# Two thirds of an attention's value projection moved ahead of its queries and keys, and made by a seven-product scheme

## The chip, the cores and the metric

The kernel runs on one core of a Trainium2 chip. The metric is device time in microseconds (us) of one execution. Engines in this text: PE (TensorE, matrix products), DVE (VectorE), ACT (ScalarE) and SP, whose queue issues the loads of weights. PE writes into PSUM, which has eight banks here (the tile `banks`, 128 x 8 x 512); DVE and ACT read results from there.

## The reference

A two-layer encoder on 256 tokens of width 2048, all in float32. Only the second layer's attention changes; in short:

```python
def dilated_attention(h, w_qkv, w_o):        # h: (1, 256, 2048)
    qkv = (h @ w_qkv).reshape(B, T, G, 3, DIL_HEADS, HEAD_DIM)   # G=3 groups, 8 heads of 128
    for g, (window, dil) in enumerate(((128, 1), (512, 4), (2048, 16))):
        q = apply_partial_rotary(qkv[:, :, g, 0], cos, sin) * (HEAD_DIM ** -0.5)
        k = apply_partial_rotary(qkv[:, :, g, 1], cos, sin)
        v = qkv[:, :, g, 2]
        o, lse = banded_attention(split(q), split(k), split(v), n_side)
        ...
    wts = softmax(stack(lses), axis=0)
    return (sum of wts * outs).reshape(B, T, 1024) @ w_o
```

`x = x + dilated_attention(rms_norm(x, g))` stands between two feed-forward blocks `x + relu(h @ w1)**2 @ w2` with 8192 hidden columns. The merge over groups equals one softmax over the 512 score columns of the three groups together, and the kernel does it so.

## The kernel before

**Float32 products from three.** Every float32 operand is split into a high part (rounded to the fp32r type) and a low part, the rest. `three` (lines 197 to 201) issues high*high, high*low, low*high. For weights the high part `wh` is a cast by ACT (L194) and the low part `wl` a subtraction by DVE (L195), each over half a step's weights, 128 x 1024.

**Steps.** The program is a list of steps; each takes one 128 x 2048 block of weights (1 MB, 512 rows by 512 columns, or 256 by 1024) and has four quarters of matmuls. The list is walked by hand in order, and every engine runs its instructions in that order. In step `i`, after each quarter `n`: the PE part of the tasks put at that quarter, the `after` list, then `prep(i + 2, n)` (which makes the parts of the weights of step `i + 2`), then the tasks' DVE and ACT work (`post`). At the end of a step come `evac`, `prep(i + 2, 3)`, `load(i + 5)` on SP and the step's `post`. `wh` and `wl` have four buffers each, so the half made in step `i` for step `i + 2` goes where a half of step `i` has just been read.

Three kinds of steps matter:

- Column form (`gemm_cols`, kind "a"): queries and keys, transposed. The weights are the stationary operand; a step issues 16 matmuls of 512 columns with `wh` (L229) and 16 of 256 with `wl` (L234). In the first step of a projection the `wl` products of quarters 2 and 3 each read both halves; in the middle ones quarter 2 reads the first half and quarter 3 the second.
- Row form (`gemm_rows`, kind "a"): values and the output projection, 24 matmuls of 512 columns.
- Pairs (`gemm_pair`): the feed-forward. A step takes 256 rows by 1024 columns. Kind "s" issues eight products by `three`, 24 matmuls. Kind "x" issues seven, by a scheme in Strassen's manner, 21 matmuls, from sums of weight blocks that DVE makes in `prep_x` (lines 166 to 188) and sums of activation blocks (`sums_and_parts`). Five banks more take part, and at the end of a call the sums are closed on DVE (`begin`, `last_sum`).

**The second attention.** After the first feed-forward, for each half `hh` of the eight heads: 24 column steps (queries and keys of the three groups, four steps each), then 12 row steps (values of the three groups). Then eight row steps of the output projection. `DilHeads` has the head tasks, for each of the four heads `h` of a half:

- `s1`: scores into a bank; its post adds the mask (L908) into `sc` and, for group 2, runs `softmax` (reduce L659, two exponentials on ACT L662, reciprocal L664, scaling L666).
- `s2`: eight transposes (L918, L920) into two banks; its post splits them on ACT and DVE (`dpT`, `dpTd`).
- `s3`: products with the values (L199 to L201 with `dpT`, then L940); its post writes `oT`, ACT L950 and then DVE L951.

In "a" steps a task's bank comes from `Banks.misc`, which hands out banks 6 and 7 in turn. With `i` the first step after the last key projection of a half, `s1` of group 2 stands at steps `i + 2` to `i + 5`, `s2` at `i + 7` to `i + 10`, `s3` at `i + 12` and `i + 13`. After each query or key projection come its turns (rotary, DVE L865 to L868): the first half at the end of the projection's last step, the second at quarter 1 of the next.

**The norm ahead of it.** `Norm` transposes chunks of `x` (L393) and scales them into `xT`; pairs 4 to 7 (chunks 2 and 3) come last, in the last step of the feed-forward and the first of the attention. With `perm` tokens are put in another order, and DVE makes the low part by `gx` (L421) and a subtraction (L423). `rows` and `rows_out` (L454), then `cols` and `cols_out`, one step apart, spread the reciprocal root; `cols` reads what `rows_out` wrote.

Of the kernel before, what the change touches and what calls it, by code (L numbers as in the profile page):

```python
# [14 lines left out]
P = 128  # L15
T = 256
# [32 lines left out]
def tile_encoder(ctx: ExitStack, tc: tile.TileContext, ins, out):  # L49
# [242 lines left out]

    def gemm_pair(w, cp, A, sums_of, order, finish, split_end=False, soon=False):
        made, q = [], {}
# [3 lines left out]
        def left(pair, which):  # L298

            t, u = A[pair // 2], 2 * (pair % 2)  # L300
            names = ("S3", "S2", "S4", "S1")[:sums_of[pair].shape[2]] if pair in sums_of else ()
            if which in names:
                c = sums_of[pair]
                return [c[:, h, names.index(which), :] for h in range(2)]
            a, ts_ = {"A11": (0, 0), "A12": (1, 0), "S1": (0, 1), "A21": (0, 1), "A22": (1, 1)}[which]
            return [t[:, u + a, h, ts_ * P:(ts_ + 1) * P] for h in range(2)]
# [67 lines left out]
    class Norm:  # L374
        def __init__(self, n, perm, pairs=(), kept=()):
            self.n, self.perm, self.kept = n, perm, kept
# [18 lines left out]
        def parts(self, c, half, halves=(0, 1)):  # L395
# [3 lines left out]
            if 2 * c + half in self.pairs:  # L399
                keep = int(2 * c + half in self.kept)  # L400
                raw = blocks()
                for a in range(2):
                    k = 4 * c + 2 * half + a
                    nc.scalar.activation(raw[:, 3 + 2 * a:5 + 2 * a, :].rearrange("p u t -> p (u t)"), self.tp[:, a, :], AF.Copy, scale=gT[:, self.n, k:k + 1])
                self.sums[2 * c + half] = part.pool.tile([P, 2, 3 + keep, P], F32R, name="xs", tag=("xs", "xk")[keep],
                                                              bufs=1 if keep else len(self.pairs) - len(self.kept))
                sums_and_parts(raw, xT, half, self.sums[2 * c + half])
                return
            for which, a in [(which, 2 * half + a) for which in ("hi", "lo") for a in halves]:
# [15 lines left out]
                else:  # L425
                    nc.vector.scalar_tensor_tensor(out=lo, in0=src, scalar=g, in1=hi.bitcast(F32),
                                                   op0=ALU.mult, op1=ALU.subtract)

        def root(self):
# [39 lines left out]

    def sums_and_parts(b, t, half, sums):  # L470

        hi, lo = (t[:, 2 * half:2 * half + 2, h, :].rearrange("p a (u t) -> p a u t", u=2) for h in range(2))
        whole = b[:, 3:7, :].rearrange("p (a u) t -> p a u t", u=2)
        keep = sums.shape[2] == 4

        def own():
            nc.scalar.copy(hi, whole)
            subtract(nc.vector, lo, whole, hi.bitcast(F32))

        if keep:  # L480
            own()
# [3 lines left out]
        if not keep:  # L485
            nc.scalar.copy(hi, whole)
        for n, src in ((slice(0, 3), b[:, 0:3, :]), (slice(3, 4), b[:, 4:5, :]))[:1 + keep]:
            nc.scalar.copy(sums[:, 0, n], src)
        if not keep:
            subtract(nc.vector, lo, whole, hi.bitcast(F32))  # L490
        for n, src in ((slice(0, 3), b[:, 0:3, :]), (slice(3, 4), b[:, 4:5, :]))[:1 + keep]:
            subtract(nc.vector, sums[:, 1, n], src, sums[:, 0, n].bitcast(F32))

# [43 lines left out]
    def at_after(i, n, f):  # L537
        later_after.append((i, n, f))
# [172 lines left out]
    def ffn(norm, w1, w2, next_norm, next_done):  # L711
        for g in range(4):
# [4 lines left out]
            def hidden(made, q, cp, hT=hT, sums=sums, pairs2=pairs2, last=last):  # L717
# [14 lines left out]
                for r in range(4):  # L732
# [10 lines left out]
                    def post(r=r, held=held):  # L743
# [3 lines left out]
                        if pair in pairs2:  # L747
# [3 lines left out]
                            def parts_of(c=c, half=half, raw=raw, pair=pair):  # L751
                                sums[pair] = part.pool.tile([P, 2, 3, P], F32R, name="hs", tag="hsum", bufs=3)
                                sums_and_parts(raw, hT[c], half, sums[pair])
                            steps[i + (3 if cp else 2 * r - 1)].after[1].append(parts_of)
# [6 lines left out]
            for cp in range(2):  # L761
                more = g and not cp
                order = ff_order(FF_PAIRS + FF_KEPT, (0, 1, 2, 5, 3, 4, 6, 7)) if more else ff_order(FF_PAIRS)
                gemm_pair(w1, 2 * g + cp, norm.xT, norm.sums, order, lambda made, q, cp=cp: hidden(made, q, cp))

# [49 lines left out]
            for cp in range(2):  # L815
                parted = last and cp == 1
                order = range(8) if last else (0, 1, 2, 4, 3, 6, 5, 7)
                if parted:
                    order = ((0, 1, 2, 4, 3, 5, 6, 7), (0, 1, 3, 2, 5, 4, 6, 7))[next_done is None]
                gemm_pair(w2g, cp, hT, sums, ff_order(pairs2, order), lambda made, q, cp=cp, parted=parted: residual(made, q, cp, parted),  # L820
                          parted, parted and next_done is not None)

    ffn(norms[1], ins["ffn0_w1"], ins["ffn0_w2"], lambda: norms[2], begin_norm(2, True))


    parts[len(steps)] = "attention"
    n2 = norms[2]
    dil_oT = [None] * 2
    rope = {}
# [20 lines left out]
    class DilHeads:  # L850
        def __init__(self, hh):
            self.hh = hh
            self.q, self.k, self.v, self.sc = {}, {}, {}, {}

# [25 lines left out]
        def v_out(self, g, acc):  # L880
            if g == 0:
                self.v[g] = split_v(acc, n2.r)
                return
            t = part.pool.tile([P, 2, 512], F32, name="v", tag="mid", bufs=9)
# [45 lines left out]
        def s3_pe(self, h):  # L930
# [4 lines left out]
            for kt in range(2):  # L935
                three(o[:, 0, :], [v[:, kt, hs] for v in self.v[0]], [hi[:, kt, :], lo[:, kt, :]], kt == 0, False)
            for g in (1, 2):
# [14 lines left out]

    wd = ins["dil_wqkv"]
    at(len(steps), None, load_rope)
    at(len(steps) + 2, None, make_rope)
    for hh in range(2):
# [3 lines left out]
        for g in range(3):  # L960
# [16 lines left out]

# [214 lines left out]
```

## Time and profile before

| | us |
|---|---|
| median of 3 runs | 2254.18 (2252.92 to 2256.74) |
| the profiled execution | 2253.24 |
| its span, first to last instruction | 2251.5 |

| stretch of the span (us) | what | PE busy | DVE busy | ACT busy |
|---|---|---|---|---|
| 640 to 1080 | first feed-forward, later part | 440.00 | 414.85 | 264.56 |
| 1080 to 1220 | queries and keys, half 0 | 140.00 | 106.53 | 61.79 |
| 1220 to 1290 | values, half 0 | 70.00 | 48.19 | 38.37 |
| 1290 to 1440 | queries and keys, half 1 | 150.00 | 101.06 | 62.86 |
| 1440 to 1510 | values, half 1 | 70.00 | 46.77 | 37.32 |

How to read it: busy time is the time in which an engine had at least one instruction in flight. Successive matmuls overlap, so a single one's duration (0.39 us for 512 columns) is longer than the distance from one to the next (0.23 us); the chain of work shows distances, the timeline durations. A timeline row has the start, the duration, engine and line, operation, what is written and read, and in brackets the idle time of the engine before it and what ended it. A row of windows has the stretch, its length, the busy time of PE, weight loads, DVE, ACT and POOL, the granted PE clock, DMA share and GB/s.

### The profile page before, as it was taken

To read this page: it belongs to the slowest core of one execution; us is meant where nothing else is said; L and a number is where in the kernel's file an instruction comes from. 1 tells how busy PE (TensorE), PEld (TensorE's weight loads), DVE (VectorE), ACT (ScalarE), POOL (GpSimd) and SP (SyncE) were. 2 spreads that over 40 slices of the span, in tenths; PEclk is the share of its full clock that TensorE was granted. 3 is DMA by queue.
4 is the path that set the end of the run, shared out by engine and by line. 5 is a ranking of instruction groups with operands and counts; after the bars stand their busy time and mean duration, and the time that the engine had idled before them with its cause. 6 is when DMAs were issued, how large, how long until landed. Compare 5 with 4: busy or idle time off the path is not lost.

```text
span 2251.5 us, 28385 instructions
## 1 busy us (share of the span) xinstructions
PE 2238.7 (99%) x10906; PEld 1883.4 (84%) x10906; DVE 1891.8 (84%) x2217; ACT 1269.2 (56%) x1582; POOL 0.7 (0%) x6
## 2 busy tenths in 40 slices
PE   9999999999999999999999999999999999999998
PEld 8888888888888888888888888888888888888886
DVE  6776666899999999989877667757999999999988
ACT  6555455665665565565444544456665665665664
POOL 0000000000000000000000000000000000000000
PEclk9999999999999999999999999999999999999999
DMA  7556554656656666665555445444666666666664
GB/s 256 177 186 192 177 180 165 203 187 209 202 188 207 200 192 206 196 190 190 209 180 186 170 169 183 172 169 151 208 201 197 199 205 192 200 204 192 204 218 136
DMA packets 110728, 430.33 MB, mean 191 GB/s; under 512 B 23872, under 2 KB 24448, under 8 KB 92160
## 3 DMA queue, kind: packets, MB, share of 16 engines
q1 hardware_dynamic: 109920, 426.82, 58.1%
q8 instruction: 85, 1.39, 0.2%
q10 hardware_dynamic: 672, 1.70, 0.2%
q14 instruction: 51, 0.42, 0.1%
HBM read 426.38 MB, written 2.10 MB: 190 GB/s over the span
## 4 chain that ended last, share of the span: by engine, by line
PE 98%; DVE 1%; ACT 1%; issue 0%; ACTq 0%; POOLq 0%; POOL 0%; DVEq 0%
PE banks L199 25%; PE banks L201 25%; PE banks L200 25%; PE banks L229 13%; PE banks L234 7%; PE banks L740 1%; PE banks L393 1%; PE banks L940 0%; PE banks L900 0%; PE banks L635 0%; PE banks L1072 0%; PE banks L918 0%; PE banks L920 0%; ACT wh L194 0%; DVE wl L195 0%
## 5 line engine op out<-in xcount | busy, mean ns | idle before, releaser
L195 DVE TENSOR_TENSOR wl<-w,wh 128x1024 fp32r<-128x1024 f32 (+1 forms) x802 | 963.1, 1217 | 235.0 <-ACT wh L194 148.3
L194 ACT CAST wh<-w 128x1024 fp32r<-128x1024 f32 (+1 forms) x802 | 824.6, 1048 | 457.0 <-PE banks L201 306.3
L199 PE MATMUL banks<-wh,xT 128*128 128x512 f32 x1074 | 423.3, 394 | 0.0
L200 PE MATMUL banks<-wl,xT 128*128 128x512 f32 x1074 | 418.7, 390 | 0.0
L201 PE MATMUL banks<-wh,xT 128*128 128x512 f32 x1074 | 418.5, 390 | 0.0
L199 PE MATMUL banks<-wh,hT 128*128 128x512 f32 x804 | 316.2, 393 | 0.0
L201 PE MATMUL banks<-wh,hT 128*128 128x512 f32 x804 | 313.2, 390 | 0.0
L200 PE MATMUL banks<-wl,hT 128*128 128x512 f32 x804 | 312.9, 389 | 0.0
L229 PE MATMUL banks<-xT,wh 128*128 128x512 f32 x1280 | 312.5, 392 | 0.0
L229 PEld LDWEIGHTS banks<-xT,wh 128*128 128x128 f32 x1280 | 233.4, 188 | 44.2 <-ACT wh L194 0.2
L180 ACT CAST hs<-sums 128x1536 fp32r<-128x1536 f32 x98 | 145.3, 1482 | 186.5 <-DVE sums L138 186.5
L201 PEld LDWEIGHTS banks<-wh,xT 128*128 128x128 f32 x1074 | 201.6, 188 | 42.2
L200 PEld LDWEIGHTS banks<-wl,xT 128*128 128x128 f32 x1074 | 201.9, 188 | 40.6 <-DVE wl L195 1.2
L199 PEld LDWEIGHTS banks<-wh,xT 128*128 128x128 f32 x1074 | 201.9, 188 | 39.7
L201 PEld LDWEIGHTS banks<-wh,hT 128*128 128x128 f32 x804 | 150.9, 188 | 31.6
L200 PEld LDWEIGHTS banks<-wl,hT 128*128 128x128 f32 x804 | 151.1, 188 | 30.3
L135 DVE TENSOR_TENSOR ls<-sums,hs 128x1536 fp32r<-128x1536 f32 x98 | 171.6, 1751 | 5.6 <-ACT hs L180 5.6
L199 PEld LDWEIGHTS banks<-wh,hT 128*128 128x128 f32 x804 | 151.0, 188 | 30.0
L234 PE MATMUL banks<-xT,wl 128*128 128x256 f32 x1280 | 172.7, 284 | 0.1
L234 PEld LDWEIGHTS banks<-xT,wl 128*128 128x128 f32 x1280 | 165.8, 191 | 6.6 <-DVE wl L195 0.6
L138 DVE TENSOR_TENSOR sums<-w 128x1024 f32<-128x1024 f32 x98 | 119.4, 1218 | 0.0
L199 PE MATMUL banks<-wh,oT 128*128 128x512 f32 x192 | 76.6, 399 | 0.0
(186 smaller groups left out, 2348.7 us busy)
## 6 DMA issues: line engine op xcount, KB each, us to landing
w<-in_ffn_w_dram SPq DMA_DIRECT2D x512, 512.0 KB, 4.7
w<-in_dil_wqkv_dram SPq DMA_DIRECT2D x72, 1024.0 KB, 4.8
w<-in_na_wqkv_dram SPq DMA_DIRECT2D x47, 1024.0 KB, 5.2
w<-in_na_wo_dram SPq DMA_DIRECT2D x16, 1024.0 KB, 4.8
w<-in_dil_wo_dram SPq DMA_DIRECT2D x8, 1024.0 KB, 4.7
bias<-in_rpb_dram SPq DMA_DIRECT2D x32, 96.0 KB, 10.0
out_dram<-x SPq DMA_DIRECT2D x8, 256.0 KB, 2.6
x<-in_x_dram SPq DMA_DIRECT2D x3, 512.0 KB, 9.0
```

The source lines that it names most:

```text
L135: engine.tensor_tensor(out=out, in0=a, in1=b, op=ALU.subtract)
L138: engine.tensor_tensor(out=out, in0=a, in1=b, op=ALU.add)
L180: nc.scalar.copy(s.hs, s.sums)
L194: nc.scalar.copy(dst_hi, src)
L195: nc.vector.tensor_tensor(out=dst_lo, in0=src, in1=dst_hi.bitcast(F32), op=ALU.subtract)
L199: nc.tensor.matmul(o, left[0], right[0], start=start, stop=False)
L200: nc.tensor.matmul(o, left[0], right[1], start=False, stop=False)
L201: nc.tensor.matmul(o, left[1], right[0], start=False, stop=stop)
L229: nc.tensor.matmul(acc[j // 2][:, j % 2, :], s.hi[a][:, j * P:(j + 1) * P], xT[k][:, a].rearrange("p h t -> p (h t)"), start=k == 0 and a ...
L234: nc.tensor.matmul(acc[j // 2][:, j % 2, :T], s.lo[a][:, j * P:(j + 1) * P], xT[k][:, a, 0, :], start=False, stop=k == nk - 1 and a == 3)
L393: nc.tensor.transpose(self.tp[:, a, tb * P:(tb + 1) * P], x[:, tb, kt * P:(kt + 1) * P], ident)
L740: nc.tensor.transpose(t[:, a, tb * P:(tb + 1) * P], q["C"][:, 2 * tb + f // 4, f % 4 * P:(f % 4 + 1) * P], ident)
```

## The change

The values of 16 of the 24 value steps move to the front of the second attention, as two calls of `gemm_pair` of eight steps each: the group 0 values of both halves (weight blocks 4 and 5), then the values of half 0 for groups 1 and 2 (blocks 10 and 16). In the first call pairs 5 and 6 are "x" steps, in the second 5, 6 and 7: five in all. The eight steps left are the row-form values of half 1 for groups 1 and 2. `gemm_pair` takes the list of its two column blocks.

```diff
+    gemm_pair(wd, (4, 5), n2.xT, n2.sums, ff_order((5, 6), (0, 1, 2, 3, 5, 4, 6, 7)), two_groups)
+    gemm_pair(wd, (10, 16), n2.xT, n2.sums, ff_order((5, 6, 7), (0, 1, 2, 5, 3, 6, 7, 4)), one_half)
+
+    s0 = len(steps)
+    parts[s0 + 1] = "attention"
+    at(s0 + 1, None, load_rope)
+    at(s0 + 2, None, make_rope)
...
-        for g in range(3):
-            acc = {}
-            made = gemm_rows(wd, g * 3072 + 2048 + hh * 512, n2.xT, range(4), acc, 0, 3)
-            made[-1].evac.append(lambda H=H, g=g, acc=acc: H.v_out(g, acc))
+        if hh:
+            for g in (1, 2):
+                acc = {}
+                made = gemm_rows(wd, g * 3072 + 2048 + hh * 512, n2.xT, range(4), acc, 0, 3)
+                made[-1].evac.append(lambda H=H, g=g, acc=acc: H.v_out(g, acc))
```

The values are written by `two_groups` (`high` on ACT, `low` on DVE, within the next call's first steps) and `one_half` (ACT):

```diff
+        for m, (tb, hh) in enumerate(QUARTERS):
+            made[-1].after[m].append(lambda tb=tb, hh=hh: last_sum(q, tb, hh, q["C"][:, 2 * tb + hh, :]))
+            at_after(i, m, lambda tb=tb, hh=hh: high(tb, hh))
+            at_after(i + (m + 1) // 4, (m + 1) % 4, lambda tb=tb, hh=hh: low(tb, hh))
```

The head tasks get steps and quarters of their own, counted from `i = begins[2]`, the first step after the half's last key projection. For half 0 these steps are now the column steps of half 1, for half 1 its eight row steps and the output projection:

```diff
+        i = begins[2]
+        S1, S2, S3 = ((((1, 1), (2, 1), (5, 1), (6, 1)), ((4, 1), (6, 3), (8, 1), (9, 1)), ((6, 1), (8, 3), (10, 1), (11, 1))),
+                      (((1, 1), (2, 1), (3, 1), (4, 1)), ((4, 3), (5, 1), (6, 1), (7, 1)), ((8, 1), (8, 3), (9, 1), (9, 3))))[hh]
...
-                at(begins[g] + 2 + h, lambda H=H, h=h, g=g: H.s1_pe(h, g), lambda H=H, h=h, g=g: H.s1_post(h, g))
+                when, n = S1[h] if g == 2 else (2 + h, 1)
+                at(begins[g] + when, lambda H=H, h=h, g=g: H.s1_pe(h, g), lambda H=H, h=h, g=g: H.s1_post(h, g), quarter=n)
...
-            at(begins[2] + 7 + h, lambda H=H, h=h: H.s2_pe(h), lambda H=H, h=h: H.s2_post(h))
-            at(begins[2] + 12 + h // 2, lambda H=H, h=h: H.s3_pe(h), lambda H=H, h=h: H.s3_post(h),
-               quarter=(1, 3)[h % 2])
+            at(i + S2[h][0], lambda H=H, h=h: H.s2_pe(h), lambda H=H, h=h: H.s2_post(h), quarter=S2[h][1])
+            at(i + S3[h][0], lambda H=H, h=h: H.s3_pe(h), lambda H=H, h=h: H.s3_post(h), quarter=S3[h][1])
```

In one quarter the tasks run in the order in which they were put: all `s1` of a half ahead of its `s2` and `s3`.

The norm makes sums for pairs 5, 6 and 7: pairs 4 to 7 are scaled by ACT into a buffer `raw`, the permutation included, and split from there by one cast and one subtraction (`own_parts`); `differences` (three subtractions) and `keep` (`sum_parts`: two casts, two subtractions) follow for 5, 6 and 7, for 5 and 6 in the next step, for 7 three steps on:

```diff
+                if self.perm:
+                    own_parts(raw, xT, half)
+                    if pair in self.kept:
+                        i = now["i"] + (3 if pair == self.kept[-1] else 1)
+                        steps[i].after[0].append(lambda: differences(raw))
+                        steps[i].after[2].append(lambda: self.keep(pair, raw))
+                    return
...
+    def own_parts(b, t, half):
+        hi, lo = ends(t, half)
+        nc.scalar.copy(hi, whole(b))
+        subtract(nc.vector, lo, whole(b), hi.bitcast(F32))
```

The values of group 0 are kept in tiles of 128 x 4 x 2 x 256, and `s3_post` writes a head's result over the values that its `s3` has read. The score tiles of heads 2 and 3 move to another pool. The rest of the diff renames and splits helpers.

More of the change, by code (lines that the diff above doesn't have):

```diff
@@ L300, in left @@
             t, u = A[pair // 2], 2 * (pair % 2)
[L301 to L304, printed above, removed]
+            if pair in sums_of and which in sums_of[pair]:
+                return sums_of[pair][which]
             a, ts_ = {"A11": (0, 0), "A12": (1, 0), "S1": (0, 1), "A21": (0, 1), "A22": (1, 1)}[which]
@@ L375, in __init__ @@
         def __init__(self, n, perm, pairs=(), kept=()):
-            self.n, self.perm, self.kept = n, perm, kept
+            self.n, self.perm, self.kept, self.own = n, perm, kept, None
             self.pairs, self.sums = pairs, {}
@@ L399, in parts @@
             if 2 * c + half in self.pairs:
-                keep = int(2 * c + half in self.kept)
+                pair = 2 * c + half
                 raw = blocks()
@@ L403, in parts @@
                     k = 4 * c + 2 * half + a
[L404 to L407, printed above, removed]
+                    src, dst = self.tp[:, a, :], raw[:, 3 + 2 * a:5 + 2 * a, :].rearrange("p u t -> p (u t)")
+                    if self.perm:
+                        src = src.rearrange("p (j s r) -> p r s j", s=4, r=4)
+                        dst = dst.rearrange("p (r s j) -> p r s j", s=4, r=4)
+                    nc.scalar.activation(dst, src, AF.Copy, scale=gT[:, self.n, k:k + 1])
+                if self.perm:
+                    own_parts(raw, xT, half)
[4 more added lines that the diff above has]
+                    return
+                own = None
+                if pair in self.kept:
+                    t = part.pool.tile([P, 2, 4, P], F32R, name="xk", tag="xk")
+                    three, own = t[:, :, :3, :], t[:, :, 3, :]
+                else:
+                    three = part.pool.tile([P, 2, 3, P], F32R, name="xs", tag="xs", bufs=3)
+                self.sums[pair] = sums_and_parts(raw, xT, half, three, own)
                 return
@@ L427, in parts, with keep @@
                                                    op0=ALU.mult, op1=ALU.subtract)
+        def keep(self, pair, raw):
+            if self.own is None:
+                self.own = part.pool.tile([P, 2, 4, P], F32R, name="xk", tag="xk")
+            three, own = part.pool.tile([P, 2, 3, P], F32R, name="xs", tag="xs", bufs=3), self.own[:, :, pair % 4, :]
+            sum_parts(raw, three, own)
+            self.sums[pair] = named(three, own)
         def root(self):
@@ L468, in blocks, with ends, whole, differences @@
         return part.pool.tile([P, 7, P], F32, name="h", tag="h", bufs=2)
[L470 to L481, printed above, removed]
+    def ends(t, half):
+        return [t[:, 2 * half:2 * half + 2, h, :].rearrange("p a (u t) -> p a u t", u=2) for h in range(2)]
+    def whole(b):
+        return b[:, 3:7, :].rearrange("p (a u) t -> p a u t", u=2)
+    def own_parts(b, t, half):
+        hi, lo = ends(t, half)
+        nc.scalar.copy(hi, whole(b))
+        subtract(nc.vector, lo, whole(b), hi.bitcast(F32))
+    def differences(b):
         subtract(nc.vector, b[:, 0:5:4, :], b[:, 3:5, :], b[:, 4:7:2, :])
@@ L484, in sums_and_parts, with sum_parts, named @@
         subtract(nc.vector, b[:, 2, :], b[:, 5, :], b[:, 1, :])
[L485 to L492, printed above, removed]
+    def sum_parts(b, sums, kept=None):
+        both = ((sums, b[:, 0:3, :]), (kept, b[:, 4, :]))[:1 + (kept is not None)]
+        for to, src in both:
+            nc.scalar.copy(to[:, 0], src)
+        for to, src in both:
+            subtract(nc.vector, to[:, 1], src, to[:, 0].bitcast(F32))
+    def named(sums, kept=None):
+        names = {name: [sums[:, h, n, :] for h in range(2)] for n, name in enumerate(("S3", "S2", "S4"))}
+        if kept is not None:
+            names["S1"] = [kept[:, h, :] for h in range(2)]
+        return names
+    def sums_and_parts(b, t, half, sums, kept=None):
+        if kept is not None:
+            own_parts(b, t, half)
+            differences(b)
+            sum_parts(b, sums, kept)
+        else:
+            differences(b)
+            hi, lo = ends(t, half)
+            nc.scalar.copy(hi, whole(b))
+            nc.scalar.copy(sums[:, 0], b[:, 0:3, :])
+            subtract(nc.vector, lo, whole(b), hi.bitcast(F32))
+            subtract(nc.vector, sums[:, 1], b[:, 0:3, :], sums[:, 0].bitcast(F32))
+        return named(sums, kept)
     def rsqrt_begin(ss):
@@ L751, in parts_of @@
                             def parts_of(c=c, half=half, raw=raw, pair=pair):
-                                sums[pair] = part.pool.tile([P, 2, 3, P], F32R, name="hs", tag="hsum", bufs=3)
-                                sums_and_parts(raw, hT[c], half, sums[pair])
+                                t = part.pool.tile([P, 2, 3, P], F32R, name="hs", tag="hsum", bufs=3)
+                                sums[pair] = sums_and_parts(raw, hT[c], half, t)
                             steps[i + (3 if cp else 2 * r - 1)].after[1].append(parts_of)
@@ L763, in ffn @@
                 order = ff_order(FF_PAIRS + FF_KEPT, (0, 1, 2, 5, 3, 4, 6, 7)) if more else ff_order(FF_PAIRS)
-                gemm_pair(w1, 2 * g + cp, norm.xT, norm.sums, order, lambda made, q, cp=cp: hidden(made, q, cp))
+                gemm_pair(w1, (4 * g + 2 * cp, 4 * g + 2 * cp + 1), norm.xT, norm.sums, order, lambda made, q, cp=cp: hidden(made, q, cp))
             w2g = w2[4 * g:4 * (g + 1)]
@@ L819, in ffn @@
                     order = ((0, 1, 2, 4, 3, 5, 6, 7), (0, 1, 3, 2, 5, 4, 6, 7))[next_done is None]
-                gemm_pair(w2g, cp, hT, sums, ff_order(pairs2, order), lambda made, q, cp=cp, parted=parted: residual(made, q, cp, parted),
+                gemm_pair(w2g, (2 * cp, 2 * cp + 1), hT, sums, ff_order(pairs2, order), lambda made, q, cp=cp, parted=parted: residual(made, q, cp, parted),
                           parted, parted and next_done is not None)
-    ffn(norms[1], ins["ffn0_w1"], ins["ffn0_w2"], lambda: norms[2], begin_norm(2, True))
-    parts[len(steps)] = "attention"
+    ffn(norms[1], ins["ffn0_w1"], ins["ffn0_w2"], lambda: norms[2], begin_norm(2, True, (4,), (5, 6, 7)))
     n2 = norms[2]
+    wd = ins["dil_wqkv"]
+    first_v = {}
     dil_oT = [None] * 2
@@ L852, in __init__ @@
             self.hh = hh
-            self.q, self.k, self.v, self.sc = {}, {}, {}, {}
+            self.q, self.k, self.v, self.sc = {}, {}, first_v[hh], {}
         def qk(self, which, g):
@@ L935, in s3_pe @@
             for kt in range(2):
-                three(o[:, 0, :], [v[:, kt, hs] for v in self.v[0]], [hi[:, kt, :], lo[:, kt, :]], kt == 0, False)
+                three(o[:, 0, :], [self.v[0][:, h, n, kt * P:(kt + 1) * P] for n in range(2)],
+                      [hi[:, kt, :], lo[:, kt, :]], kt == 0, False)
             for g in (1, 2):
```

42 lines of the change are left out of this document (30 added, 12 removed).

## The prediction

> **What bounds the kernel now.** I read the page first, then the waits of PE, then the chain of work in order of time, then the timelines of DVE around the second attention.
>
> ```profile
> PE 2238.7 (99%) x10906; PEld 1883.4 (84%) x10906; DVE 1891.8 (84%) x2217; ACT 1269.2 (56%) x1582; POOL 0.7 (0%) x6
> ...
> PE 98%; DVE 1%; ACT 1%; issue 0%; ACTq 0%; POOLq 0%; POOL 0%; DVEq 0%
> ```
>
> The waits of PE, all of them (us in total, times, longest):
>
> ```profile
> PE banks L1072 <- POOL ident masks.py:199: 1.4, 1, 1.4
> PE banks L393 <- DVE xT L426: 0.8, 1, 0.8
> PE banks L393 <- DVE x L516: 0.3, 1, 0.3
> PE banks L445 <- DVE rw L440: 0.3, 1, 0.3
> ```
>
> TensorE is the bound from end to end and waits 2.8 us in 2251.5; none of it lies between the first projection of the second attention and its last head task. So a matmul taken out is worth its full time, a wait put in costs its full time, and DVE (84%) has slack only on average. This row, of windows over the first feed-forward, shows DVE at 94% with PE never idle:
>
> ```profile
> 640.00:1080.00 440.00, 440.00 (x1988) 363.45 (x1987) 414.85 (x446) 264.56 (x302) 0.00 (x0) 1.00 0.61 197
> ```
>
> **The change part by part.**
>
> *The products.* Timeline of PE, the first matmul of three successive steps: an "x" step (21 matmuls), an "s" step (24), the next.
>
> ```profile
> 1064.28 0.39 PE L199 MATMUL banks<-wh,hT 128*128 128x512 f32 x1
> ...
> 1069.04 0.39 PE L199 MATMUL banks<-wh,hT 128*128 128x512 f32 x1
> ...
> 1074.48 0.39 PE L199 MATMUL banks<-wh,hT 128*128 128x512 f32 x1
> ```
>
> 4.76 us against 5.44, so 0.68 us per "x" step. A row-form value step has 24 such matmuls, as an "s" step has. Five "x" steps: **-3.4 us**. The other transposes and head products keep their counts. This is the only term that takes time away.
>
> *DVE in the 16 steps.* From the groups:
>
> ```profile
> L195 DVE TENSOR_TENSOR wl<-w,wh 128x1024 fp32r<-128x1024 f32 (+1 forms) x802 | 963.1, 1217 | 235.0 <-ACT wh L194 148.3
> ...
> L135 DVE TENSOR_TENSOR ls<-sums,hs 128x1536 fp32r<-128x1536 f32 x98 | 171.6, 1751 | 5.6 <-ACT hs L180 5.6
> ...
> L138 DVE TENSOR_TENSOR sums<-w 128x1024 f32<-128x1024 f32 x98 | 119.4, 1218 | 0.0
> ...
> L138 DVE TENSOR_TENSOR sums<-sums,w 128x512 f32<-128x512 f32 x98 | 67.8, 692 | 3.3
> L138 DVE TENSOR_TENSOR w<-sums,w 128x512 f32<-128x512 f32 x98 | 67.8, 692 | 3.3
> ```
>
> and from the list of all groups:
>
> ```profile
> L135 DVE TENSOR_TENSOR C<-banks,C 128x512 f32<-128x512 f32 x48 | 32.8, 684 | 0.0
> ...
> L571 DVE SCALAR_TENSOR_TENSOR v<-banks,rstd,v 128x512 fp32r<-128x512 f32 x12 | 8.5, 747 | 0.8 <-ACT v L569 0.8
> ```
>
> An "s" step costs DVE 2 x 1.22 = 2.4 us, an "x" step 2.4 + 1.75 + 1.22 + 2 x 0.69 = 6.8. The second call (5 s, 3 x) is 32.5 us, with the closing sums of a call (one of 1024 columns, 1.22, and six of 512, 0.69: 5.4) and the four `low` (0.75 each, as L571) 40.9, against 5 x 5.44 + 3 x 4.76 = 41.5 us of PE. The first call (6 s, 2 x) is 33.6 with its sums, and some 10 us of norm work, against 43.8 of PE. That is 98 to 100%, a little above the 94% of the feed-forward; weights are made two steps ahead, and at each "x" step I find 1 to 2 us in hand. I take **0** here; if the cover went, each late us would be a us of PE (ends 0 and +4).
>
> *The norm.* Ahead of `rows_out`, pairs 4 to 7 lose four operations each and gain a subtraction each, two sets of differences and a kept sum:
>
> ```profile
> 1081.18 0.48 DVE L421 TENSOR_SCALAR gx<-banks,gT 128x256 f32<-128x256 f32 x1
> ...
> 1082.89 0.68 DVE L138 TENSOR_TENSOR x<-x,banks 128x512 f32<-128x512 f32 x1
> ...
> 1094.99 0.41 DVE L454 COPY rbc<-banks 128x256 f32<-128x256 f32 x1
> ```
>
> Four pairs at 1.71 (1081.18 to 1082.89) are 6.8 us; in their place come four subtractions of 512 columns (2.7), two sets of differences (1.0 each, an estimate from four 128-column operations at a quarter of 0.69 and some start) and 0.8: 5.5. So 1.3 less work, but every pair now waits for two scalings and a cast on ACT, which I put at 0.65 of DVE idle a pair, 2.6. `cols` waits for this copy. So it ends near 1095.40 + 1.3 = 1096.7, while PE, from 1080.97, gets to `cols` after two "s" steps, the half of a third, eight transposes and `rows` (1080.97 + 13.6 + 0.9 + 0.4 = 1095.9): **+0.9 us**, ends 0 (as before, 1095.40) and 2.
>
> *Heads of half 0.* They leave row-form steps for the column-form steps of half 1, where another rule holds. Chain of work, then DVE's timeline, at head products that already stood in such steps:
>
> ```profile
> 1291.89 3.63 PE banks L229 x16
> ...
> 1297.13 1.91 PE banks L234 x16
> ...
> 1305.04 0.89 PE banks L940 x8
> 1305.93 1.91 PE banks L234 x16
> ```
>
> ```profile
> 1298.65 1.22 DVE L195 TENSOR_TENSOR wl<-w,wh 128x1024 fp32r<-128x1024 f32 x1 [3.84 <-PE banks L234]
> ...
> 1306.98 1.23 DVE L195 TENSOR_TENSOR wl<-w,wh 128x1024 fp32r<-128x1024 f32 x1 [3.71 <-PE banks L234]
> 1308.12 0.42 DVE L951 TENSOR_TENSOR oT<-banks,oT 128x256 fp32r<-128x256 f32 x1
> ```
>
> A column-form step is 3.63 + 1.91 us; `s3` is 1.61 (1297.13 - 1291.89 - 3.63). The `wl` that DVE makes at quarter 1 needs the buffer that L234 still reads: it starts at 1306.98, behind the half of L234 that ends at 1305.93 + 0.96, and in the first step of a projection in the middle of the second half (1298.65). The head task's DVE work stands behind it. Nothing waits in before, since a bank comes back a step later. Now the softmax, DVE's timeline of half 1:
>
> ```profile
> 1446.02 2.34 DVE L195 TENSOR_TENSOR wl<-w,wh 128x1024 fp32r<-128x1024 f32 x2
> ...
> 1451.48 1.23 DVE L195 TENSOR_TENSOR wl<-w,wh 128x1024 fp32r<-128x1024 f32 x1 [1.49 <-ACT wh L194]
> 1452.62 0.42 DVE L908 TENSOR_TENSOR sc<-banks,dmask 128x256 f32<-128x256 f32 x1
> ...
> 1456.88 2.35 DVE L195 TENSOR_TENSOR wl<-w,wh 128x1024 fp32r<-128x1024 f32 x2
> 1459.15 0.42 DVE L908 TENSOR_TENSOR sc<-banks,dmask 128x256 f32<-128x256 f32 x1
> ...
> 1473.53 0.42 DVE L908 TENSOR_TENSOR sc<-banks,dmask 128x256 f32<-128x256 f32 x1
> ```
>
> From mask to the next work 4.26 us, period 6.53. Step 6 after the last key projection gets, at quarter 1, `s1` of head 3 and `s3` of head 0, and at quarter 3 `s2` of head 1, which takes both of the two banks that the former two wrote. From the end of quarter 1: PE does 0.44 + 1.61 + 1.91 and wants the banks at 3.97. DVE starts `wl` at 3.1, the mask at 4.25, ends the softmax at 8.5, and only then subtracts `s3`'s low part, to 8.95. PE gets two transposes (0.22) in between: 4.8 us with DVE on time. DVE isn't: from the first of these key steps on it has three `wl`, `s2`'s subtraction, a turn (2.7) with its parts, and head 2's softmax, 13.4 us and a late start of 0.8 for 13.2 us of PE; 0.9 late: **+5.7**. Ends: 1.0 (were `wl` not held, mask at 0.5, all done at 5.2) and 6.6.
>
> At step 8, `s2` of head 2 at quarter 1 and `s3` of head 1 at quarter 3 share a bank. The step is a projection's first: `wl` starts 0.4 us before PE's quarter 3 ends, 1.14 later the subtraction of 0.68 reads the bank: **+1.5**, ends 0 and 2.2.
>
> *Heads of half 1.* The four softmaxes start a step earlier, in four steps on end of 5.9 us against DVE's 6.53. Chain, `s1` of the first and the last head before:
>
> ```profile
> 1450.37 0.44 PE banks L900 x4
> ...
> 1468.07 0.44 PE banks L900 x4
> ```
>
> In after the first is at 1450.37 - 5.45 = 1444.92, behind the turns that end at 1446.02; masks at 1448.28 and every 6.53 us, the fourth at 1467.87, read by 1468.29. PE did that head's `s1` at 1462.62, and at quarter 3 of the same step, 3.17 later, wants its bank for `s2` of head 0, whose first two transposes go ahead: 2.3 us. `s2` of head 1 then comes half a step later, while the subtraction that frees its first bank follows the fourth softmax (1472.8, against PE at 1471.75): 1.1. **+3.4**, ends 0 and 5.
>
> *At nothing.* 16 more DMA issues on SP: each step loads two halves of 512 KB for one of 1024, the same bytes, five steps ahead of use. Rope tables are loaded a step nearer to their use: the DMA list has 4.0 us to landing, the step is 5.56; late, they would hold DVE by the difference.
>
> ```profile
> w<-in_ffn_w_dram SPq DMA_DIRECT2D x512, 512.0 KB, 4.7
> w<-in_dil_wqkv_dram SPq DMA_DIRECT2D x72, 1024.0 KB, 4.8
> ...
> rope_c<-in_rope_c_dram ACTq DMA_DIRECT2D x1, 32.0 KB, 4.0
> ```
>
> Sum: -3.4 + 0.9 + 5.7 + 1.5 + 3.4 = **+8.1 us**. The profiled execution took 2253.24 (span 2251.5 and 1.7 around it), so 2261.3; it stands 0.9 under the median of 2254.18, from which the sum gives **2262.3**.
>
> **The rivals.**
>
> *The banks are free in time (not slower).* Place: quarter 3 of steps 6 and 8. It decides if DVE's and ACT's reads end within 2 us of PE's write. Then only -3.4 is left: 2250.8. For it: PE waits for no bank in before. Against it: the low part above came 2.2 us after its `s3` ended (1305.93 to 1308.12) without a softmax ahead, and the fourth mask 5.5 us after its `s1` (1468.07 to 1473.53). If the one wait of PE for x (0.3) goes too, 2250.5.
>
> *Part of them.* With the low ends of 1.0, 0 and 0 and with 4.8, 1.5 and 0 the net is -2.4 to +2.9: 2251.8 to 2257.1. For it: ends worked from a queue that I ordered by hand.
>
> *The clock falls after the wait.* At step 6 PE stands for some 4 us on end. The trace has the clock lower where PE does little, at its end, and its first transposes at half the rate of the others (20 in 4.4 us; eight of L940's, as large, in 0.89):
>
> ```profile
> 2240.00:2251.00 11.00, 1.46 (x7) 0.88 (x5) 4.41 (x13) 4.08 (x10) 0.00 (x0) 0.70 0.51 191
> ```
>
> ```profile
> L1072 PE MATMUL banks<-ident 128*128 128x128 f32 x20 | 4.4, 389 | 1.4 <-POOL ident masks.py:199 1.4
> ```
>
> Half rate for as long as at the start, some 4 us, costs 2 more: 2264.3. Against it: after the start no wait of PE reaches 1 us, so nothing here shows how long one must be. [...]
>
> *DVE runs out in the "x" steps.* At 98 to 100% a lateness of over 2 us reaches PE in each of five: 2262 + 4 to 10.
>
> **How the numbers follow.** About 0.2% (4.5 us) is what a measurement of this kernel tells from no change. Forecast, net above +4.5: 0.58; clock: 0.07; DVE runs out: 0.03; so slower 0.68. Part: 0.14, banks free: 0.12, within 0.2%: 0.26. No row carries more than -3.7, so the 0.06 for faster is for what I haven't seen. The likeliest one's own range is 2258 to 2266. To leave out no more than 2 in 10 I go down through the partial case to 2252.5, and up to the high ends of the four waits together (-3.4 + 2 + 6.6 + 2.2 + 5 = 12.4), 2266.6.
>
> **What would show it.** The waits of PE should have rows for `s2`'s transposes (old L918, L920) on DVE's `oT` and `sc`, some 5 to 6 us in one place, and for `s3` on `dpT`, 1.5; PE should have 15 matmuls fewer, 10891. If PE's waits stay under 3 us, the banks were free, and the prediction is wrong by 11 us. If DVE's `wl` shows up as releaser of PE in the value steps, my 0 for them is wrong.

## The result, and the profile after

The changed kernel takes 2265.83 us (median of 6 runs, 2265.39 to 2266.53) where the kernel before takes 2254.21: a ratio of 1.0052, 95% interval 1.0039 to 1.0064. It is slower by 11.6 us; the forecast was 2262.3 in a range of 2252.5 to 2266.6. Its profiled execution has a span of 2263.6 us, 12.1 more than before. The engines of the page, then the waits of PE (us in total, times, longest):

```profile
PE 2240.5 (99%) x10891; PEld 1883.0 (83%) x10891; DVE 1922.5 (85%) x2254; ACT 1281.6 (57%) x1599; POOL 0.7 (0%) x6
```

```profile
PE banks L960 <- DVE v L990: 3.8, 1, 3.8
PE banks L960 <- DVE sc L948: 3.4, 1, 3.4
PE banks L958 <- DVE sc L948: 1.6, 1, 1.6
PE banks L199 <- DVE dpT L195: 1.5, 1, 1.5
...
PE banks L479 <- DVE rbc L474: 0.3, 1, 0.3
```

15 matmuls are gone (10906 to 10891), and five waits have come: L958 and L960 are `s2`'s transposes, L199 with `dpT` is `s3`, L479 is `cols`. All five were in the forecast; the second wait that it had in half 1 (1.1 us, at `s2` of head 1) did not come. Before, PE had none between the first projection of the second attention and its last head task. The rest of the list is that of before, to 0.1 us.

A measure that leaves out small differences elsewhere in the span: the stretch from the end of the last product of the first feed-forward (the last row of PE that reads its `hT`) to the start of the first such row in the second. It is 1646.80 - 1080.54 = 566.3 us before and 1659.17 - 1080.65 = 578.5 after: +12.3. All that follows is in that stretch.

**Step 6 of half 0.** The chain of work in order of time, then DVE's timeline. (L229 and L234 are the products of the step, L939 is `s1`, L199 to L201 and L981 are `s3`; on DVE and ACT, L948 is the mask, L700 the reduce, L703 the exponentials, L707 the scaling, and L990 the subtraction behind `s3`.)

```profile
1341.21 3.65 PE banks L229 x16
1344.87 0.44 PE banks L939 x4
...
1346.03 0.89 PE banks L981 x8
1346.92 0.97 PE banks L234 x8
...
1347.92 2.08 DVE wl L195 x2
...
1350.37 1.23 DVE m L700
...
1351.63 1.53 ACT sc L703 x4
...
1353.38 0.88 DVE sc L707 x2
...
1354.65 0.69 PE banks L960 x2
...
1356.19 3.41 PE banks L229 x8
1359.61 1.06 PE banks L234 x8
1360.67 1.84 PE banks L229 x8
```

```profile
1347.64 2.36 DVE L195 TENSOR_TENSOR wl<-w,wh 128x1024 fp32r<-128x1024 f32 x2
1349.92 0.42 DVE L948 TENSOR_TENSOR sc<-banks,dmask 128x256 f32<-128x256 f32 x1
...
1353.38 0.88 DVE L707 TENSOR_SCALAR sc<-sc,sum 128x512 f32<-128x512 f32 x2
1354.17 0.42 DVE L990 TENSOR_TENSOR v<-banks,v 128x256 fp32r<-128x256 f32 x1
```

The chain leaves PE here for the only time between the norm and the end of half 0's heads' softmaxes: `wl`, mask, reduce, exponentials, scaling, and behind them the subtraction L990 that frees `s3`'s bank. Without a wait the next step would start at 1341.21 + 3.65 + 0.44 + 1.61 + 1.92 + 0.87 = 1349.7. It starts at 1356.19.

The last three rows of that chain show something more. Eight matmuls of 512 columns take 3.41 us, and a moment later 1.84: PE ran at half rate after the wait. The windows have the granted clock (the column of 0.69 and 0.54; stretch, length, busy time of PE, weight loads, DVE, ACT, POOL, clock, DMA share, GB/s):

```profile
1351.00:1356.00 5.00, 1.35 (x7) 1.35 (x8) 1.97 (x5) 1.97 (x6) 0.00 (x0) 0.69 0.41 174
1356.00:1360.00 4.00, 4.00 (x13) 3.23 (x13) 1.92 (x2) 1.82 (x3) 0.00 (x0) 0.54 0.00 0
...
1500.00:1505.00 5.00, 5.00 (x21) 4.06 (x21) 3.18 (x6) 4.36 (x9) 0.00 (x0) 0.69 0.16 66
```

**Half 1** (the last of these rows). Chain, PE's matmuls behind the wait at half rate (0.43 each in the place of 0.23):

```profile
1498.32 0.44 PE banks L960 x2
1499.98 0.43 PE banks L199
...
1502.54 0.43 PE banks L199
```

The waits as distances between the ends of successive matmuls, less the usual distance of that form: 1.8 + 4.2 = 6.0 at step 6, 1.8 at step 8, 3.6 in half 1, 0.6 at `cols`, 11.9 in all; the slow matmuls 2.3 behind step 6 and 1.6 in half 1. (The list of waits counts from the end of the matmul in flight, so each is some 0.2 to 0.4 less.) 11.9 + 3.9 - 3.4 = 12.4, against 12.3 measured.

### The profile page after: what moved, and what is told of

It reads as the page before. It is cut to its first block, busy times and chain, and to the rows that moved or that the text cites. A ratio compares the mean times of both kernels' runs of the same rounds, so it can differ in the third digit from the quotient of the medians.

```text
span 2263.6 us, 28441 instructions
## 1 busy us (share of the span) xinstructions
PE 2240.5 (99%) x10891; PEld 1883.0 (83%) x10891; DVE 1922.5 (85%) x2254; ACT 1281.6 (57%) x1599; POOL 0.7 (0%) x6
## 4 chain that ended last, share of the span: by engine, by line
PE 97%; DVE 1%; ACT 1%; issue 0%; DMA 0%; ACTq 0%; SPq 0%; DVEq 0%
PE banks L199 25%; PE banks L201 25%; PE banks L200 25%; PE banks L229 13%; PE banks L234 7%; PE banks L781 1%; PE banks L391 1%; DVE wl L195 0%; PE banks L981 0%; PE banks L676 0%; PE banks L939 0%; ACT wh L194 0%; DMA w<-in_na_wqkv_dram 0%; PE banks L960 0%; ACT sc L703 0%
## 5 line engine op out<-in xcount | busy, mean ns | idle before, releaser
L199 PE MATMUL banks<-wh,xT 128*128 128x512 f32 x1049 | 414.1, 395 | 0.0
L200 PE MATMUL banks<-wl,xT 128*128 128x512 f32 x1049 | 409.6, 390 | 0.0
L201 PE MATMUL banks<-wh,xT 128*128 128x512 f32 x1049 | 409.4, 390 | 0.0
L199 PE MATMUL banks<-wh,hT 128*128 128x512 f32 x804 | 316.2, 393 | 0.0
L229 PE MATMUL banks<-xT,wh 128*128 128x512 f32 x1280 | 314.0, 394 | 0.1
L201 PE MATMUL banks<-wh,hT 128*128 128x512 f32 x804 | 313.2, 390 | 0.0
L229 PEld LDWEIGHTS banks<-xT,wh 128*128 128x128 f32 x1280 | 234.5, 189 | 44.8 <-ACT wh L194 0.4
L180 ACT CAST hs<-sums 128x1536 fp32r<-128x1536 f32 x103 | 152.7, 1483 | 197.3 <-DVE sums L138 197.3
L201 PEld LDWEIGHTS banks<-wh,xT 128*128 128x128 f32 x1049 | 197.3, 188 | 41.6
L199 PEld LDWEIGHTS banks<-wh,xT 128*128 128x128 f32 x1049 | 197.4, 188 | 38.9
L135 DVE TENSOR_TENSOR ls<-sums,hs 128x1536 fp32r<-128x1536 f32 x103 | 180.4, 1752 | 5.5 <-ACT hs L180 5.5
L201 PEld LDWEIGHTS banks<-wh,hT 128*128 128x128 f32 x804 | 150.9, 188 | 31.8
L199 PEld LDWEIGHTS banks<-wh,hT 128*128 128x128 f32 x804 | 151.0, 188 | 29.8
L234 PE MATMUL banks<-xT,wl 128*128 128x256 f32 x1280 | 172.9, 284 | 0.0
L234 PEld LDWEIGHTS banks<-xT,wl 128*128 128x128 f32 x1280 | 165.7, 191 | 6.7 <-DVE wl L195 0.9
L138 DVE TENSOR_TENSOR sums<-w 128x1024 f32<-128x1024 f32 x103 | 125.5, 1218 | 0.0
L138 DVE TENSOR_TENSOR C<-C,banks 128x1024 f32<-128x1024 f32 (+1 forms) x88 | 75.2, 889 | 3.6 <-DVE C L135 0.5
```

The source lines that it names most:

```text
L135: engine.tensor_tensor(out=out, in0=a, in1=b, op=ALU.subtract)
L138: engine.tensor_tensor(out=out, in0=a, in1=b, op=ALU.add)
L180: nc.scalar.copy(s.hs, s.sums)
L199: nc.tensor.matmul(o, left[0], right[0], start=start, stop=False)
L200: nc.tensor.matmul(o, left[0], right[1], start=False, stop=False)
L201: nc.tensor.matmul(o, left[1], right[0], start=False, stop=stop)
```

## The experiments

My theory: PE waits for banks where head tasks come half a step after another on the same bank, because DVE frees them behind `wl` and a softmax; a long wait also lowers the clock. The main rivals: the time lies in the 16 value steps, and the slow matmuls have another cause than PE's standing still.

**Tasks apart, both halves** (`e1_apart`).

```diff
-        S1, S2, S3 = ((((1, 1), (2, 1), (5, 1), (6, 1)), ((4, 1), (6, 3), (8, 1), (9, 1)), ((6, 1), (8, 3), (10, 1), (11, 1))),
-                      (((1, 1), (2, 1), (3, 1), (4, 1)), ((4, 3), (5, 1), (6, 1), (7, 1)), ((8, 1), (8, 3), (9, 1), (9, 3))))[hh]
+        S1, S2, S3 = ((((1, 1), (2, 1), (5, 1), (6, 1)), ((4, 1), (7, 1), (8, 1), (9, 1)), ((5, 3), (10, 1), (11, 1), (12, 1))),
+                      (((1, 1), (2, 1), (3, 1), (4, 1)), ((5, 3), (6, 3), (7, 1), (7, 3)), ((8, 1), (8, 3), (9, 1), (9, 3))))[hh]
```

> The changed kernel with its head tasks put so that none comes within half a step of a task on the same bank: half 0 s2 of head 1 at step 7, s3 at (5,3), (10,1), (11,1), (12,1); half 1 s2 at (5,3), (6,3), (7,1), (7,3). Theory (PE waits for banks, and runs at half clock after the two long waits): the 11.3 us of bank waits and the 3.9 us of slow matmuls go, only the 15 products saved and some 0.5 at cols are left: 2265.8 - 15.2 = 2250.6 us. Rival (the time lies in the 16 value steps moved ahead, in their DVE work or loads): the time stays above 2262. Rival (other waits take their place, since DVE's work is the same): 2254 to 2260, with new rows in the waits of PE.

Measured: 2249.74 us against 2253.52 for before on the same chip, ratio 0.9984 (0.9975 to 0.9993). The waits of PE from 1080 to 1560 us, all of them:

```profile
PE banks L479 <- DVE rbc L474: 0.3, 1, 0.3
```

The stretch is 1643.38 - 1080.00 = 563.4 us, 15.1 below the changed kernel and 2.9 below before: -3.4 for the products, +0.6 at `cols`. So the whole loss, and the half-rate matmuls with it, hung on where the head tasks stood. The rival of the 16 value steps is out but for that 0.6. (The median is 3.8 below before; some 1 us of it lies outside the stretch, in parts that were not changed.)

**Tasks apart in half 0 only** (`e2_half0_apart`): the first of the two lines above alone.

> As e1_apart, but half 1 stays as in the changed kernel. Theory: the waits of 6.0 and 1.8 us and the 2.3 us of slow matmuls after the first go, the wait of 3.6 and its 1.6 of slow matmuls stay: 2265.8 - 10.1 = 2255.7 us. If the two halves' waits were not separate (half 1 late because half 0 was), it would be near 2250.6; if half 0 is not the place, near 2265.8.

Measured: 2255.15 us, ratio 1.0008 (0.9998 to 1.0017). The waits of PE:

```profile
PE banks L960 <- DVE sc L948: 3.4, 1, 3.4
...
PE banks L958 <- DVE dpT L195: 0.9, 1, 0.9
```

and the windows over this wait and behind it:

```profile
1485.00:1490.00 5.00, 1.72 (x11) 1.55 (x12) 3.91 (x4) 1.93 (x3) 0.00 (x0) 1.00 0.46 143
1490.00:1495.00 5.00, 4.11 (x23) 3.21 (x22) 3.68 (x6) 4.85 (x10) 0.00 (x0) 1.00 0.16 69
```

The halves are separate: half 0 goes, half 1's 3.4 stays. The expectation was wrong in its parts, and the sum came out by luck, since 1.6 less and 1.1 more nearly cancel: the clock stayed at 1.00 behind the same wait of 3.4 us, and instead the second wait of half 1 came (L958 on `dpT`, 0.9 in the list, 1.1 as a distance). In the changed kernel that wait was hidden: PE, at half rate, reached it 1.6 us later.

**The waits filled** (`e3_filled`), the schedule as in the changed kernel.

```diff
             p = self.sc[h // 2][:, h % 2]
+            for n in range({(0, 1): 50, (1, 0): 32}.get((self.hh, h), 0)):
+                nc.tensor.transpose(banks[:, 2 * ((ps.pair + 1) % 3), n % 4 * P:(n % 4 + 1) * P], ident, ident)
             self.pt = [ps.misc() for _ in range(2)]
```

> The changed kernel with 50 transposes of the identity into an idle bank ahead of half 0's s2 of head 1, and 32 ahead of half 1's s2 of head 0: 5.5 and 3.5 us of PE work in the place of waits of 6.2 and 3.8, nothing else changed (work that the kernel does not need). If the slow matmuls behind the waits come from PE standing still (clock granted by its activity): they go, the time is 2265.8 - 3.9 = 2261.9 us. If they come from something else, as DVE and ACT reading PSUM or late weights: they stay, 2265.8 us or up to 0.5 more.

Measured: 2262.58 us, ratio 1.0041 (1.0027 to 1.0055), span 2260.4, 3.2 below the changed kernel (2.9 in the stretch, 575.6). The clock over the two filled places:

```profile
1353.00:1358.00 5.00, 4.86 (x35) 4.28 (x33) 2.86 (x6) 2.13 (x4) 0.00 (x0) 1.00 0.01 3
1494.00:1499.00 5.00, 5.00 (x35) 4.33 (x33) 3.34 (x6) 2.08 (x6) 0.00 (x0) 1.00 0.63 211
```

No slow matmul is left, with the same work on DVE, ACT and the loads. So here the slow rate came from PE's standing still. The 3.9 us are gone and half 1's second wait (1.1) is back, as in the run before.

**`s3` ahead of `s1`** (`e4_s3_first`): the loop that puts `s2` and `s3` stands ahead of the one that puts `s1`.

> The changed kernel with s2 and s3 of a half put ahead of its s1, which swaps one pair of tasks only: at step 6 of half 0, s3 of head 0 comes ahead of s1 of head 3, so that DVE subtracts s3's low part ahead of the softmax. Theory: the wait there falls from 6.0 to about 1 us (mask read at 5.0 after the end of quarter 1, PE there at 4.0), too short for the clock to fall: 2265.8 - 5.0 - 2.3 = 2258.5 us. If the banks alone counted and not the softmax in DVE's queue, the time stays 2265.8.

Measured: 2260.42 us, ratio 1.0028 (1.0017 to 1.0038), span 2257.0, 6.6 below the changed kernel; 2258.5 was expected. At step 6 one wait is left:

```profile
PE banks L958 <- DVE v L990: 1.5, 1, 1.5
```

As a distance it is 1.8 where I said 1.0: DVE comes to `wl` late, behind head 2's softmax, as in the changed kernel (1347.64 there). So of the 6.0 us some 4.2 were the softmax ahead of the subtraction, and the rest `wl` and DVE's lateness; with the softmax out of the way the wait was too short to lower the clock. The order of this one pair is worth 6.4 us in the stretch of the profiled executions (578.5 against 572.1) and 5.4 us between the medians.

**The waits filled in part** (`e5_part_filled`): 24 and 10 transposes.

> The changed kernel with 24 transposes of the identity (2.6 us) ahead of half 0's s2 of head 1 and 10 (1.1 us) ahead of half 1's s2 of head 0, in an idle bank: PE then stands about 3.3 us on end in half 0 (4.2 before) and 2.5 in half 1 (3.6). If the clock falls for a wait of over about 3.4 us only: neither is followed by slow matmuls, and the second wait of half 1 (1.1 us, as in e2_half0_apart) comes back: a span near 2263.6 - 3.9 + 1.1 = 2260.8 us. If 2.5 us is enough: slow matmuls behind both, 2263.6.

Measured once: 2267.18 us, span 2265.0, over both of the expected spans. The stretch is 578.6, that of the changed kernel; 1.3 us of the rest were lost by the end of the first feed-forward (1082.00 for 1080.65), in parts that are the same. The two filled places in the waits of PE (the two added lines make L962 of L960), and the clock:

```profile
PE banks L962 <- DVE v L992: 3.0, 1, 3.0
PE banks L962 <- DVE sc L948: 2.3, 1, 2.3
...
```

```profile
1358.00:1362.00 4.00, 4.00 (x13) 3.32 (x12) 1.91 (x2) 1.41 (x2) 0.00 (x0) 0.50 0.13 18
1499.00:1504.00 5.00, 3.64 (x18) 2.79 (x18) 3.34 (x6) 2.51 (x7) 0.00 (x0) 1.00 0.64 213
```

A wait of 3.0 us was followed by a fall of the clock, one of 2.3 was not. My figure of 3.4 was too high, and with the run of half 0 apart, where the clock stayed at 1.00 behind 3.4 us, the length of a wait alone does not decide.

What else decides can be read from the traces. In the changed kernel the clock changes at 1352.88, 1359.71, 1499.66 and 1503.07, and each distance from one change to the next is a whole number of times 3.413 us (2, 41 and 1). So here are windows of that length that begin and end at these places (or a whole number of lengths away): in the changed kernel at step 6, then in half 1, and then over the wait of 3.4 us with half 0 apart (counted back from 2247.62, where the clock of that run falls at its end).

```profile
1349.47:1352.88 3.41, 0.44 (x2) 0.20 (x2) 2.09 (x3) 1.25 (x3) 0.00 (x0) 1.00 0.78 291
1352.88:1356.30 3.42, 1.65 (x7) 1.65 (x8) 1.38 (x4) 1.02 (x5) 0.00 (x0) 0.50 0.04 17
1356.30:1359.71 3.41, 3.41 (x10) 2.65 (x10) 1.92 (x2) 1.52 (x3) 0.00 (x0) 0.50 0.00 0
```

```profile
1496.24:1499.66 3.42, 1.34 (x9) 1.26 (x10) 3.25 (x4) 0.35 (x2) 0.00 (x0) 1.00 0.56 165
1499.66:1503.07 3.41, 3.41 (x9) 2.65 (x9) 1.71 (x5) 3.31 (x7) 0.00 (x0) 0.50 0.34 144
```

```profile
1483.03:1486.45 3.42, 1.87 (x10) 1.31 (x8) 1.97 (x4) 3.41 (x6) 0.00 (x0) 1.00 0.07 29
1486.45:1489.86 3.41, 1.58 (x10) 1.46 (x11) 2.99 (x4) 0.35 (x1) 0.00 (x0) 1.00 0.61 185
```

The same wait of half 1 leaves PE 1.34 us of work in one of these lengths in the changed kernel, and the clock falls at its end; with half 0 apart the wait lies across two lengths, PE works for 1.87 and 1.58 us in them, and the clock stays. The other three falls at a wait follow lengths with 1.24 us of PE's work (half 1 of the run before this one, where 1490 to 1495 has a clock of 0.81), 1.30 (this run) and 0.78 (the six "x" steps below); the 2.3 us of this run lay across two as well, 0.75 and 1.55. So in these runs the clock fell where PE stood for some 2.1 us or more of one such length, and not for 1.8 or less. By these bounds (an estimate) a wait of 2.3 us that lies within one length could lower the clock too; none here lay so.

**Two "x" steps** (`e6_two_x`), on the version with tasks apart: `ff_order((6,), ...)` in both calls.

> e1_apart with two x steps in the place of five (pair 6 alone in both calls): nine matmuls of 512 columns more and three x steps less of DVE work. If each x step is worth its three matmuls, 0.68 us, and nothing else: 2.0 us above e1_apart, near 2251.7 where before is 2253.5. If DVE's work for x steps costs time somewhere in these 16 steps: less than that, down to no difference.

Measured: 2251.84 us, ratio 0.9991 (0.9982 to 1.0001). The stretch is 565.4 us, 2.0 above that version's 563.4 (1645.87 - 1080.47 of PE's rows): three "x" steps are worth 2.0, so 0.67 each and 3.4 for five, and DVE's work for them costs nothing.

**Six "x" steps** (`e7_six_x`), on the version with tasks apart: the first call with `ff_order((5, 6, 7), (0, 1, 2, 5, 3, 6, 7, 4))`.

> e1_apart with six x steps: the first call gets pairs 5, 6 and 7, in the order of the second (s s s x s x x s). If DVE has room: 0.7 us under e1_apart, near 2249.1. By the ledger DVE then has some 48 us of work in the 43 us of the first call: it runs out by some 5 us, of which two steps of lead cover part; PE then waits for wl, ls or the cols chain, 2 to 4 us above e1_apart, with DVE as releaser in the value steps.

Measured: 2254.77 us, ratio 1.0002 (0.9993 to 1.0012). The one new thing in the waits of PE, and the clock behind it:

```profile
PE banks L479 <- DVE rbc L474: 2.9, 1, 2.9
```

```profile
1099.00:1105.00 6.00, 6.00 (x16) 4.84 (x17) 4.23 (x6) 1.38 (x2) 0.00 (x0) 0.50 0.26 59
```

The stretch is 568.3, 5.0 above five "x" steps: 2.7 more wait at `cols` (3.2 as a distance), since the sums of the early "x" step stand ahead of `rows_out` on DVE, and 2.9 of half rate behind it, less the 0.7 saved. That is over the 2 to 4 that were expected, by the half rate, which does not come each time: the ten executions lie between 2251.63 us, with a mean granted clock of 0.999, and 2256.22, with 0.998. No `wl` or `ls` is waited for.

**`cols` a step later** (`e8_cols_later`), on the version with tasks apart: `at(i + 4, ...)` for `at(i + 3, ...)`.

> e1_apart with cols one step later. If the wait of 0.5 us at cols is the last cost of the moved norm: it goes, the span is 0.5 us shorter (2247.0) and the waits of PE have no row for cols; nothing else waits for it, since the values read its result five steps on. If DVE is merely late there and everything behind shifts, another wait takes its place.

Measured: 2249.77 us against 2254.33, ratio 0.9981 (0.9971 to 0.9991). The row of `cols` is gone from the waits, and the stretch is 1644.63 - 1081.85 = 562.8, 0.6 less. (The span is 2248.7, longer than expected: this execution had lost 1.9 us by the end of the first feed-forward, 1081.85 for 1080.00, in parts that are the same. The medians do not show the 0.6: 2249.77 here, 2249.74 with `cols` in its old place.) This is the version that beats both kernels by most in the stretch, 3.5 us under before.

**Six "x" steps with `cols` later** (`e9_six_x_later`): on the last, `ff_order((5, 6, 7), (0, 1, 2, 3, 5, 6, 7, 4))`.

> e8_cols_later with a sixth x step, the first call in the order s s s s x x x s, so that no x step's sums stand on DVE ahead of what cols waits for. If the wait at cols was all that the sixth x step cost in e7_six_x: PE waits nowhere in the value steps, and the stretch from the last product of the first feed-forward to the first of the second feed-forward's second matrix is 562.8 - 0.7 = 562.1 us; near 2249 us where before is 2254. If three x steps on end are more than DVE's lead covers (3 x 6.8 us of DVE in 3 x 4.8 of PE, six us late against two steps of lead): PE waits for ls or wl in the third or behind it, 1 to 4 us, 563 to 566 us for the stretch.

Measured: 2252.31 us, ratio 0.9989 (0.9980 to 0.9999).

```profile
PE banks L200 <- DVE wl L195: 1.2, 1, 1.2
PE banks L199 <- DVE rstd L484: 0.7, 1, 0.7
```

The stretch is 1647.06 - 1082.00 = 565.1: the sixth step loses 2.3 where it should win 0.7. Three "x" steps on end use up DVE's lead, and `wl` is waited for at the end of them; L199 waits for the read of the bank that `cols` now holds when the first "x" step wants it. As distances the two are 1.4 and 1.0. Six steps fail in both orders that were run; the order of `e7_six_x` together with the later `cols` was not run, so whether DVE can carry six is open.

## Why the prediction was right, and where its sizes were off

| term | forecast | measured | where |
|---|---|---|---|
| five "x" steps | -3.4 | -3.4 | three of them 2.0 (two "x" steps) |
| wait at `cols` | +0.9 | +0.6 | gone with `cols` later |
| DVE in the 16 steps | 0 | 0 | no PE wait on `wl` or `ls` |
| step 6, half 0 | +5.7 | +6.0 | gone with the tasks apart |
| step 8, half 0 | +1.5 | +1.8 | the same |
| half 1 | +2.3 + 1.1 | +3.6 + 0 | half 0 apart: 3.6 + 1.1 |
| half rate behind waits | a rival, +2 at 0.07 | +3.9 | gone with the waits filled |
| sum | +8.1 | +12.4 (before rounding) | stretch: +12.3 |

The mechanism, the places and the releasers came out as worked: the waits of the tasks on DVE's `v` (the tile that now holds `oT`), `sc` and `dpT`, and none elsewhere. That 2265.83 lies in the range, 0.8 under its upper end, is in part luck: that end was made of the high ends of the four waits. The waits came within 0.3 us of their middle values (half 1 by luck too: its first wait was 1.3 over, its second of 1.1 did not come), and the half rate, which the sum left out, took the room up to the end. What was mis-sized:

- *The clock.* The forecast had the rival right in kind, and gave it 0.07. It was the larger part of the miss: 3.9 of 4.3 us. The step that failed is "nothing here shows how long one must be": the trace of before could not price it, and I let that stand for unlikely. I also looked for it behind step 6 alone; the wait of half 1 set it off as well. The size was near, 2 for the 2.3 of step 6. The mean granted clock is 0.996 or 0.997 in all six executions of the changed kernel, and 0.999 in all four with the waits filled, so it fell in each of the six. The runs show that a wait may or may not be followed by half rate (3.4 us: yes in the changed kernel, no with half 0 apart), and that a length of 3.413 us need not be idle for it: one with 1.34 us of PE's work was followed by a fall. With transposes of the identity in the two places the clock stayed at 1.00 (the windows of `e3_filled`).
- *Half 1.* 3.6 for 2.3. I took DVE's period of 6.53 us for all four softmaxes. The third period of the changed kernel is 7.6 (mask at 1490.23, then 1497.85), as DVE waited for ACT. Its rows, then two of before:

```profile
1493.36 1.24 ACT L926 ACTIVATE v<-banks,rstd 128x512 f32<-128x512 f32 x2
...
1495.57 2.36 DVE L195 TENSOR_TENSOR wl<-w,wh 128x1024 fp32r<-128x1024 f32 x2 [1.00 <-ACT wh L194]
```

```profile
1462.29 1.25 ACT L569 ACTIVATE v<-banks,rstd 128x512 fp32r<-128x512 f32 x2
...
1467.00 0.42 DVE L908 TENSOR_TENSOR sc<-banks,dmask 128x256 f32<-128x256 f32 x1
```

  In each pair the first row is ACT's timeline, the second DVE's. The group 1 values are scaled on ACT at the end of step 3, between the exponentials and the cast of `wh` for which DVE's `wl` waits. The trace of before had such a period already: two scalings, of the group 0 values, stand at the same place there, and that mask comes 7.85 us after the one before it (1459.15). I read the period from two other masks. With one long period in three, the 2.3 would have been 3.4 to 3.6 (an estimate, 1.1 or 1.3 more).
- *The ledger of DVE.* I had it at 98 to 100% in the 16 steps. Windows of the changed kernel over them:

```profile
1081.00:1168.00 87.00, 86.70 (x391) 71.59 (x391) 79.17 (x99) 52.09 (x65) 0.00 (x0) 1.00 0.62 205
```

  79.2 of 87 us, 91% (weights are made two steps ahead, so these are not quite the steps' own work). I summed durations, and successive operations of DVE overlap: two `wl` on end take 2.36 us, not 2.43, and a subtraction of 512 columns is followed by the next operation after 0.6 us for a duration of 0.67 (1341.66, then 1342.27). The 0 that I took was right for five steps; with three "x" steps on end it was not.

The rivals: "the banks are free in time" and "part of them" are out, by the waits of the changed kernel. "DVE runs out" did not come with five "x" steps; with three on end it came, with 1.4 us at `wl` and 1.0 at the bank of `cols`.

## What to carry to other kernels

Where PE is the bound, a task's place is good or bad by when the other engines give back its buffer, not by PE's own count: write down, for each bank, the last reader, what stands ahead of that reader in its engine's queue, and which of that waits for PE itself. Here a saving of 3.4 us in products was real and lost four times over to two banks; the order of two posts was worth 6.4 us, nine other places for the tasks 15 (both in the stretch).

Price a wait on PE of some 3 us or more at its length and, where the clock falls, at the half rate behind it, 1.6 to 2.9 us in these runs; by the bounds above a wait of over 4.2 us would lower it wherever it lies (an estimate, twice 2.1). If the wait can't be moved, PE work that nobody needs, put into it, can save that part: here 3.9 us of slow matmuls went, 2.9 us of the stretch.

## What the runs showed of the hardware

After a wait of PE of 2.9 us (six "x" steps), 3.0 (the waits filled in part), 3.4 (half 1 of the changed kernel, and with `s3` ahead of `s1`) and 3.8 (step 6 of the changed kernel) the granted clock fell to 0.50. The half rate cost 2.3 us at step 6, 1.6 in half 1 of the changed kernel and 2.9 with six "x" steps. With half 0 apart it stayed at 1.00 behind a wait of 3.4 us, as it did behind 2.3 us with the waits filled in part. In the changed kernel the clock changed only at whole multiples of 3.413 us from one another (2, 41 and 1 around its two long waits). At a wait it fell after lengths in which PE worked for 0.44 to 1.34 us, not after those with 1.58 and 1.87 us (half 0 apart).

It stayed at 0.50 for one length (3.41 us) in half 1 of the changed kernel, where PE worked through all of it. It stayed for two (6.83 us) at step 6, with the waits filled in part and with six "x" steps, where PE worked for 1.65, 2.53 and 3.16 us of the first; what settles that is open. In half 1 the fall came 1.3 us after PE had gone back to work (1498.32, then 1499.66), so the slow matmuls need not be the first ones behind a wait. In the kernel before it could not be seen at a wait, since between 30 and 2200 us none was longer than 0.3 us.
